# HGRN2's normed output copied by DMA into a tile typed as rounded fp32, transposed there, and the first heads' transposes placed behind the second heads' products

## The chip, the cores and the metric

The kernel runs on one core of a Trainium2 chip. The metric is the device time of one execution in microseconds (us); of several runs the median is given. The engines are named as the profile names them: PE (TensorE) multiplies, PEld is its load of the stationary operand, DVE (VectorE), ACT (ScalarE) and POOL (GpSimd) work on elements, and SP (SyncE) issues most of the DMAs. ACT and POOL issue DMAs too, and in such a case the profile writes ACTq or POOLq.

## The reference, cut to what matters

One decoder layer on 256 tokens of width 1024: two token mixers read one input projection, their outputs are projected, gated, added, projected again and normalised, and a feed-forward block follows. The change is in the first mixer, at the place where its output `o_a` is normed and gated and handed to `w_branch_a`:

```python
o_a = hgrn2_mixer(hq, hf, hi, lb)                     # B, S, 8 heads, 128
y_a = rms_norm(o_a, hgrn_norm_w) * silu(hg)           # per head
z_a = einsum('bsc,cd->bsd', y_a, w_branch_a)
z_b = einsum('bsc,cd->bsd', moba(...), w_branch_b)
mixed = einsum('bsc,cd->bsd', g_a * z_a + g_b * z_b, w_out)
```

## The kernel before

Large products are made of three: both operands are split into a high part, which is the value in the type of rounded fp32 (`F32R`, in the rows fp32r), and a low part, the rest. Weights arrive from HBM as tiles of 1024 KB (`raw`, issued by SP, L230), ACT casts the high part (`wh`, L236), DVE subtracts the low part (`wl`, L238), and PE uses both. Up to three tiles are staged ahead of their use. Beside them SP and POOL build sums of weights in HBM (`sums`, L246, L247, L252) for later products.

The tokens lie in two tiles of 128 (index `u`). The first mixer is a generator, `hgrn_steps`, and the second, attention, is one too (`moba_heads`); the big projections call `side.step()` at fixed places, and each call runs a generator up to its next `yield`. In this stretch the projections are `mk` and `mq` (keys and queries of the attention, `wide_pair`, L363 and L366: per step one product of 512 columns and one of 256), then `mv` (values, L423 to L425, 512 columns) and again `mk`. Which instruction of an engine comes first is decided at build time by a scheduler that estimates when operands are ready; on the chip every engine then works through its own list in order.

The end of `hgrn_steps` works on two groups `g` of four heads. For each group and token tile, plain fp32 products `o` (L661, L662; each shows as two records of PE) give the output, ACT squares it (`sq`, L664), DVE sums the squares and POOL takes the power -0.5 (L668), and DVE writes the normed and gated output `on` (L671). Then PE transposes `on`, 128 by 128, against the identity matrix `ident`, which lies in the tile of constants `cst` (`ot`, L680: 16 in all, eight for each group), and ACT and DVE make the high and low parts `yah` and `yal` with the norm's weights (L683, L684). Their only reader is `za`, the product with `w_branch_a`.

PSUM tiles come from two pools of four banks, `mm` for projections and `aux` for the rest. SBUF tiles of 1024 KB (`slot`) come from one pool of 12.

Of the kernel before, what the change touches and what calls it, by code (L numbers as in the profile page):

```python
# [10 lines left out]
F32 = mybir.dt.float32  # L11
F32R = mybir.dt.float32r
# [5 lines left out]
P = 128  # L18
T = 256
NT = T // P  # L20
# [115 lines left out]
def hybrid_layer_kernel(ctx: ExitStack, tc, x, xw, vecs, bias, wts, ln1_w, ln1_b, ln2_w, ln2_b, consts, out):  # L136
    nc = tc.nc
    pool = lambda name, bufs, **kw: ctx.enter_context(tc.tile_pool(name=name, bufs=bufs, **kw))
    cp = pool("cp", 1)
# [7 lines left out]
    aux = pool("aux", 4, space=PSUM)  # L147

    def slot(name, dt=F32):
        return big.tile([P, 2048], dt, tag="s8", name=name)  # L150

    def r32(ap):
        return ap.bitcast(F32)
# [166 lines left out]
    ident = cst[:, C_ID:C_ID + P]  # L320
# [2 lines left out]
    sin = cst[:, C_SIN:C_SIN + T]  # L323
    masks = msk.bitcast(U32).rearrange("p (l t) -> p l t", l=LEVELS)
    ones = cp.tile([P, P], F32R, tag="ones", name="ones")
    half = cp.tile([P, 4], F32, tag="half", name="half")

    nw = vec[:, 16:24]
# [204 lines left out]
    def hgrn_steps():  # L533
# [113 lines left out]
        for g in range(2):  # L647
# [2 lines left out]
                nc.tensor.matmul(ps[:, a, :], Kt[:, 0, 4 * g + a, :], Qt[:, 1, 4 * g + a, :], start=True, stop=True)  # L650
            nc.scalar.copy(SL[:, 4 * g:4 * g + 4, :], ps)
        yield
        on = slot("on").rearrange("p (t d) -> p t d", t=NT)
        for g in range(2):
            for u in range(NT):
                ps = aux.tile([P, 4, P], F32, tag="aux", name=f"o{g}{u}")
                for a in range(4):
                    h = 4 * g + a
                    hd = slice(h * P, (h + 1) * P)
                    if u == 1:  # L660
                        nc.tensor.matmul(ps[:, a, :], SL[:, h, :], hv[:, 0, hd], start=True, stop=False)  # L661
                    nc.tensor.matmul(ps[:, a, :], SD[:, u, h, :], hv[:, u, hd], start=(u == 0), stop=True)  # L662
                sq = sm.tile([P, 4, P], F32, tag="sg", name=f"sq{g}{u}")
                nc.scalar.activation(sq, ps, AF.Square)  # L664
                st = sm.tile([P, 12], F32, tag="ost", name=f"ost{g}{u}")
                nc.vector.reduce_sum(st[:, 0:4], sq, axis=mybir.AxisListType.X)
                nc.vector.tensor_scalar(st[:, 4:8], st[:, 0:4], 1.0 / P, RMS_EPS, op0=ALU.mult, op1=ALU.add)
                nc.gpsimd.tensor_tensor(st[:, 8:12], st[:, 4:8], half, op=ALU.pow)  # L668
                for a in range(4):
                    hd = slice((4 * g + a) * P, (4 * g + a + 1) * P)  # L670
                    nc.vector.scalar_tensor_tensor(on[:, u, hd], ps[:, a, :], st[:, 8 + a:9 + a], hgs[:, u, hd],  # L671
                                                   op0=ALU.mult, op1=ALU.mult)
            yield
            for j in range(2):
                h0 = 4 * g + 2 * j
                pt = aux.tile([P, 2, T], F32, tag="aux", name=f"ot{g}{j}")
                for a in range(2):
                    for u in range(NT):
                        hd = slice((h0 + a) * P, (h0 + a + 1) * P)
                        nc.tensor.transpose(pt[:, a, u * P:(u + 1) * P], on[:, u, hd], ident)  # L680
                for a in range(2):
                    h = h0 + a
                    nc.scalar.activation(yah[:, h, :], pt[:, a, :], AF.Copy, scale=nw[:, h:h + 1])  # L683
                    nc.vector.scalar_tensor_tensor(yal[:, h, :], pt[:, a, :], nw[:, h:h + 1], r32(yah[:, h, :]),  # L684
                                                   op0=ALU.mult, op1=ALU.subtract)
        yield

    class Steps:
# [15 lines left out]

    side = Steps()
    side.gens.append(hgrn_steps())
    side.step()

# [355 lines left out]
    def new_room():  # L1064
        return slot("room").rearrange("p (n b t) -> p n b t", n=2, b=8)
# [82 lines left out]
    with tc.manual_schedule(engines={ET.PE, ET.DVE, ET.Activation}):  # L1148
        a = new_room()
# [22 lines left out]
        d = new_room()  # L1172
# [70 lines left out]
        for i, q in enumerate(SEQUENCE):  # L1243
            if q in FAST:
                fast(q)
                if q == FAST[-1]:
                    with tc.issue_after(state["load"].ins):
                        wb2 = bcast("wb2", ln2_w, ln2_b, nc.sync)
                        unit = slot("unit")[:, 0:P]
# [131 lines left out]
```

## Time and profile before

| | |
|---|---|
| median of 3 runs | 484.13 us (484.08 to 484.2) |
| the profiled execution | 484.45 us, its span 482.6 us |
| PE busy | 476.5 us, 99% |
| DVE, ACT, POOL busy | 394.4, 302.9, 83.2 us |
| DMA moved | 131.31 MB, 272 GB/s |

The profiled execution's own time is 1.85 us longer than its span (what lies around the span) and 0.3 us above the median. A row of the timeline or of the chain begins with the start and the length in us from the start of the span.

### The profile page before, as it was taken

What the parts mean: (1) busy time and instruction counts of PE and PEld (TensorE: products, weight loads), DVE (VectorE), ACT (ScalarE), POOL (GpSimd) and SP (SyncE); (2) the same over time, 40 slices, a digit from 0 to 9 for tenths busy, and PEclk for the clock granted to TensorE, in tenths of its full rate; (3) what the DMA queues carried; (4) which work ended last, traced back from release to release, by engine and by line L of the source; (5) the groups of instructions that cost most, each with busy time, mean ns of one, the idle gap of its engine ahead of it and who ended that gap; (6) DMA issues with size and microseconds to landing.
All of it is one profiled execution on the core that took longest, in us unless ns stands there. A gap on an engine that the chain in (4) does not pass through costs nothing.

```text
span 482.6 us, 7450 instructions
## 1 busy us (share of the span) xinstructions
PE 476.5 (99%) x2915; PEld 406.7 (84%) x2915; DVE 394.4 (82%) x488; ACT 302.9 (63%) x408; POOL 83.2 (17%) x93
## 2 busy tenths in 40 slices
PE   9999999999999999999999999999999999999995
PEld 8888888788899888888888888888888888888884
DVE  4889895599977898999576678857797999889995
ACT  6699564454776677764934453643864876578744
POOL 0001111111008653440120210020010110000021
PEclk9999999999999999999999999999999999999999
DMA  8989989989699997959999986399499989789932
GB/s 301 414 304 324 292 241 270 321 249 246 208 368 238 271 239 230 235 132 338 317 267 313 289 237 244 125 316 356 173 313 320 263 294 308 242 305 379 411 99 88
DMA packets 29619, 131.31 MB, mean 272 GB/s; under 512 B 3344, under 2 KB 4752, under 8 KB 20112
## 3 DMA queue, kind: packets, MB, share of 16 engines
q1 hardware_dynamic: 20160, 113.66, 64.5%
q0 software_dynamic: 9136, 16.78, 21.6%
q8 instruction: 23, 0.38, 0.3%
q10 hardware_dynamic: 288, 0.39, 0.2%
q14 instruction: 12, 0.10, 0.0%
HBM read 128.72 MB, written 28.31 MB: 325 GB/s over the span
## 4 chain that ended last, share of the span: by engine, by line
PE 97%; DMA 1%; ACT 0%; DVE 0%; issue 0%; DVEq 0%; POOL 0%; POOLq 0%; SPq 0%; ACTq 0%
PE fu L363 5%; PE fg L363 5%; PE hq L363 3%; PE wp L1214 3%; PE wp L1215 3%; PE wp L1213 3%; PE fg L366 3%; PE fu L366 3%; PE mq L363 2%; PE mk L363 2%; PE gb L423 2%; PE mv L423 2%; PE hg L423 2%; PE hq L366 2%; PE hf L397 2%; PE ga L423 2%
## 5 line engine op out<-in xcount | busy, mean ns | idle before, releaser
L238 DVE TENSOR_TENSOR wl<-raw,wh 128x2048 fp32r<-128x2048 f32 (+1 forms) x65 | 149.0, 2297 | 42.3 <-ACT wh L236 42.0
L236 ACT CAST wh<-raw 128x2048 fp32r<-128x2048 f32 (+1 forms) x65 | 122.2, 1886 | 43.2 <-DMA raw<-in_wts_dram 18.5
L252 POOL DMA_DIRECT2D sums<-sums x26 | 21.4, 834 | 157.8 <-DMA sums<-in_wts_dram 80.2
L363 PE MATMUL fg<-x1p,wh 128*128 128x512 f32 x112 | 39.3, 395 | 0.0
L252 POOL DMA_DIRECT2D sums<-in_wts_dram x26 | 23.5, 1101 | 91.6 <-DMA sums<-in_wts_dram 91.5
L363 PE MATMUL fu<-x1p,wh 128*128 128x512 f32 x112 | 39.3, 395 | 0.0
L366 PE MATMUL fu<-x1p,wl 128*128 128x256 f32 x112 | 30.9, 278 | 0.0
L366 PE MATMUL fg<-x1p,wl 128*128 128x256 f32 x112 | 30.8, 278 | 0.0
L295 DVE TENSOR_TENSOR wlsums<-rawsums,whsums 128x2048 fp32r<-128x2048 f32 x11 | 25.2, 2289 | 6.3 <-ACT whsums L292 6.3
L292 ACT CAST whsums<-rawsums 128x2048 fp32r<-128x2048 f32 x11 | 21.1, 1917 | 8.2 <-PE wp L1215 4.9
L363 PEld LDWEIGHTS fu<-x1p,wh 128*128 128x128 f32 x112 | 20.9, 188 | 4.8
L363 PEld LDWEIGHTS fg<-x1p,wh 128*128 128x128 f32 x112 | 20.9, 188 | 4.6
L281 DVE TENSOR_TENSOR wlcorners<-rawcorners,whcorners 128x1536 fp32r<-128x1536 f32 x13 | 22.8, 1753 | 0.9 <-ACT whcorners L278 0.9
L363 PE MATMUL hq<-xp,wh 128*128 128x512 f32 x64 | 22.2, 394 | 0.0
L366 PEld LDWEIGHTS fg<-x1p,wl 128*128 128x128 f32 x112 | 21.1, 188 | 0.2
L366 PEld LDWEIGHTS fu<-x1p,wl 128*128 128x128 f32 x112 | 21.0, 188 | 0.1
L278 ACT CAST whcorners<-rawcorners 128x1536 fp32r<-128x1536 f32 x13 | 19.3, 1487 | 0.7
L366 PE MATMUL hq<-xp,wl 128*128 128x256 f32 x64 | 17.7, 277 | 0.0
L363 PE MATMUL mq<-xp,wh 128*128 128x512 f32 x48 | 17.0, 398 | 0.0
L363 PE MATMUL mk<-xp,wh 128*128 128x512 f32 x48 | 16.7, 395 | 0.0
L363 PEld LDWEIGHTS hq<-xp,wh 128*128 128x128 f32 x64 | 12.0, 188 | 2.8
L366 PE MATMUL mq<-xp,wl 128*128 128x256 f32 x48 | 13.2, 281 | 0.0
(413 smaller groups left out, 1381.2 us busy)
## 6 DMA issues: line engine op xcount, KB each, us to landing
raw<-in_wts_dram SPq DMA_DIRECT2D x63, 1024.0 KB, 7.8
sums<-in_wts_dram SPq DMA_DIRECT2D x26, 512.0 KB, 9.6
rawsums<-sums SPq DMA_DIRECT2D x11, 1024.0 KB, 6.7
rawcorners<-in_wts_dram SPq DMA_DIRECT2D x13, 768.0 KB, 7.3
sums<-in_wts_dram POOLq DMA_DIRECT2D x26, 256.0 KB, 9.9
sums<-sums POOLq DMA_DIRECT2D x26, 256.0 KB, 8.0
xw<-in_xw_dram SPq DMA_DIRECT2D x6, 640.0 KB, 9.0
raw<-sums SPq DMA_DIRECT2D x4, 512.0 KB, 7.3
```

The costliest lines, as they stand in the source:

```text
L236: nc.scalar.copy(h[:, ks, :], raw[:, ks, :])
L238: eng.tensor_sub(l[:, ks, :], raw[:, ks, :], r32(h[:, ks, :]))
L252: nc.gpsimd.dma_start(s[:, n, :], src, accum_op=ALU.add)
L278: nc.scalar.copy(h, b[:, 1:4, :])
L281: nc.vector.tensor_sub(l, b[:, 1:4, :], r32(h))
L292: nc.scalar.copy(h[:, bs, :], z)
L295: nc.vector.tensor_sub(l[:, bs, :], z, r32(h[:, bs, :]))
L363: nc.tensor.matmul(ps, wh[:, k, wcol], a.both(k), start=(k == 0), stop=False)
L366: nc.tensor.matmul(ps[:, 0, :], wl[:, k, wcol], a[0, k, slice(0, T)], start=False, stop=(k == KC - 1))
L423: nc.tensor.matmul(pss[t], ah[:, kk, ts], wh[:, k, :], start=(kk == 0), stop=False)
L1213: nc.tensor.matmul(ps, ah[:, a, :], wh[:, b, :], start=(q == begins[id(ps)]), stop=False)
L1214: nc.tensor.matmul(ps, ah[:, a, :], wl[:, b, :], start=False, stop=False)
```

## The change

The identity is copied once into a tile `unit_r` typed as rounded fp32. `on` is no longer the operand of the transposes: for each group and token tile a DMA issued by ACT copies its 128 by 512 elements word for word into a second tile `onr`, whose type is rounded fp32, and the transposes read `onr` and `unit_r` and write a PSUM tile of that type. The rows of the generator are cut in two functions. `outputs(0)` comes first, then a `yield`, then `outputs(1)` and `transposed(0)`, a `yield`, and `transposed(1)`.

```diff
+    unit_r = cp.tile([P, P], F32R, tag="unit", name="unitr")
...
+        nc.scalar.copy(unit_r, ident)
         on = slot("on").rearrange("p (t d) -> p t d", t=NT)
-        for g in range(2):
+        onr = slot("onr", F32R).rearrange("p (t d) -> p t d", t=NT)
+        def outputs(g):
             for u in range(NT):
                 ps = aux.tile([P, 4, P], F32, tag="aux", name=f"o{g}{u}")
...
-            yield
+                own = slice(4 * g * P, 4 * (g + 1) * P)
+                nc.scalar.dma_start(r32(onr[:, u, own]), on[:, u, own])
+
+        def transposed(g):
             for j in range(2):
                 h0 = 4 * g + 2 * j
-                pt = aux.tile([P, 2, T], F32, tag="aux", name=f"ot{g}{j}")
+                pt = aux.tile([P, 2, T], F32R, tag="aux", name=f"ot{g}{j}")
                 for a in range(2):
                     for u in range(NT):
                         hd = slice((h0 + a) * P, (h0 + a + 1) * P)
-                        nc.tensor.transpose(pt[:, a, u * P:(u + 1) * P], on[:, u, hd], ident)
+                        nc.tensor.transpose(pt[:, a, u * P:(u + 1) * P], onr[:, u, hd], unit_r)
+                pt = r32(pt)
...
+        outputs(0)
+        yield
+        outputs(1)
+        transposed(0)
+        yield
+        transposed(1)
         yield
```

The change moves instructions on PE, ACT and DVE; the lists of SP and POOL stay as they were. These are PE's instructions at the first group's transposes before (`mq` is the projection around them, `o` the second group's products):

```order
L680 MATMUL ot_1619<-cst,on 128x128 [waits DMAHW7_49,DVE_49]
L363 MATMUL mq_1695<-xp_97,wh_1390 128x512
L366 MATMUL mq_1695<-xp_97,wl_1391 128x256
L680 MATMUL ot_1628<-cst,on 128x128 [waits DVE_49]
L363 MATMUL mq_1695<-xp_97,wh_1390 128x512
L662 MATMUL o_1637<-hv,SD 128x128 [waits DVE_49,Activation_49]
L680 MATMUL ot_1619<-cst,on 128x128 [waits DVE_49]
L680 MATMUL ot_1619<-cst,on 128x128
```

And this is the same place of the change:

```order
L686 MATMUL ot_1660<-unitr,onr 128x128 [waits DMAHW1_49,DVE_49,Activation_49]
L686 MATMUL ot_1669<-unitr,onr 128x128 [waits DVE_49,Activation_49]
L364 MATMUL mq_1702<-xp_98,wh_1391 128x512
L367 MATMUL mq_1702<-xp_98,wl_1392 128x256
L364 MATMUL mq_1702<-xp_98,wh_1391 128x512
L686 MATMUL ot_1660<-unitr,onr 128x128 [waits DMAHW2_49]
L686 MATMUL ot_1660<-unitr,onr 128x128 x2
L686 MATMUL ot_1669<-unitr,onr 128x128 x3
L367 MATMUL mq_1702<-xp_98,wl_1392 128x256
L424 MATMUL mv_0_1749<-wh_1469,xp_97 128x512 [waits Activation_49]
```

The second group's products now stand as one block between `mk` and `mq`, ahead of this place, and the first transposes come after 14 of the 16 steps of `mq`, where it was ten. The first two wait for a DMA (the copy of token tile 0), the next six for another (token tile 1). The second group's eight stand in the next `mk` (behind all of `mv`), in the same form.

On ACT, at the same time in the program, the change has this, where before the two copies `rtk` followed `zk` directly:

```order
L781 COPY zk_1568<-mk_1594 128x256 [waits PE_49]
L677 DMA onr<-on 128x512 [waits DVE_49]
L677 DMA onr<-on 128x512 [waits DMAHW2_49,DVE_49]
L203 CAST keys<-kT 128x256 [waits PE_49]
L203 CAST keys<-kT 128x256
L786 COPY rtk_1615<-zk_1568 64x512 [waits DVE_49]
L787 COPY rtk_1615<-zk_1568 64x512
```

The two copies of the first group are issued one behind the other, and wait there for DVE's `on`. Those of the second group stand further on, one ahead of and one behind the cast of `mv`:

```order
L787 COPY rtq_1723<-zq_1678 64x512
L677 DMA onr<-on 128x512 [waits DVE_49]
L203 CAST mv<-mv_0_1749 128x512 [waits PE_49]
L677 DMA onr<-on 128x512 [waits DVE_49]
L236 CAST wh_1847<-raw_1846 128x2048 [waits DMAHW3_49,PE_49]
```

So the second of them is issued only when PE has finished the first half of `mv`. At the start of the program ACT also gets the copy of the identity, and it stands ahead of the copies that empty the first PSUM banks:

```order
L236 CAST wh_352<-raw_351 128x1024 [waits DMAHW5_49]
L654 CAST unitr<-cst 128x128 [waits DMAHW7_49]
L438 COPY Fg<-hf_145 128x2x128 [waits PE_49]
L438 COPY Fg<-hf_146 128x2x128 [waits PE_49]
L236 CAST wh_365<-raw_364 128x2048 [waits DMAHW6_49,Activation_49]
```

It waits for the DMA that brings the constants, which no instruction of ACT waited for at this place before.

## Rows read from the trace of the kernel before

**Rows 1.** The page: busy time of each engine, and the chain's shares.

```profile
PE 476.5 (99%) x2915; PEld 406.7 (84%) x2915; DVE 394.4 (82%) x488; ACT 302.9 (63%) x408; POOL 83.2 (17%) x93
PE 97%; DMA 1%; ACT 0%; DVE 0%; issue 0%; DVEq 0%; POOL 0%; POOLq 0%; SPq 0%; ACTq 0%
```

**Rows 2.** PE's waits, 5 to 470 us: total, times, longest.

```profile
PE hf L394 <- ACT fh L203: 0.2, 1, 0.2
```

**Rows 3.** Chain of work in order of time: start, us, what.

```profile
10.54 0.96 PE hf L400 x8
11.50 1.84 PE hf L397 x8
...
154.46 0.23 PE mq L363
...
158.97 0.66 PE ot L680 x6
159.62 0.67 PE o L662 x6
...
163.82 0.24 PE mv L424
...
228.84 0.23 PE za L424
```

**Rows 4.** The tile `ot`: duration min/median/max in ns, first and last start.

```profile
L680 PE MATMUL ot<-cst,on x16: 270/272/273, 157.8 to 174.7; 128*128 128x128 f32 x16
L684 DVE SCALAR_TENSOR_TENSOR yal<-ot,vec,yah x8: 473/476/483, 160.8 to 180.5; 128x256 fp32r<-128x256 f32 x8
```

**Rows 5.** Timeline of ACT, 140 to 186 us.

```profile
154.39 1.91 ACT L236 CAST wh<-raw 128x2048 fp32r<-128x2048 f32 x1 [0.62 <-PE mk L363]
156.19 0.37 ACT L767 COPY zk<-mk 128x256 f32<-128x256 f32 x1
...
171.83 0.59 ACT L203 CAST mv<-mv 128x512 fp32r<-128x512 f32 x1 [0.40 <-PE mv L425]
```

**Rows 6.** Timeline of DVE, 140 to 186 us.

```profile
154.22 2.16 DVE L671 SCALAR_TENSOR_TENSOR on<-o,ost,hgs 128x128 f32<-128x128 f32 x8
156.33 2.29 DVE L238 TENSOR_TENSOR wl<-raw,wh 128x2048 fp32r<-128x2048 f32 x1
...
168.12 2.15 DVE L671 SCALAR_TENSOR_TENSOR on<-o,ost,hgs 128x128 f32<-128x128 f32 x8
```

**Rows 7.** DMA issues, all and by stretch: KB each, us to landing.

```profile
out_dram<-z ACTq DMA_DIRECT2D x1, 256.0 KB, 2.3
...
sums<-in_wts_dram POOLq DMA_DIRECT2D x1, 256.0 KB, 6.1
...
sums<-in_wts_dram POOLq DMA_DIRECT2D x2, 256.0 KB, 9.6
```

**Rows 8.** Tile `z`: the one DMA that ACT issues at the end.

```profile
L1338 ACTq DMA_DIRECT2D out_dram<-z x1: 354/354/354, 478.5 to 478.5; - x1
```

**Rows 9.** Stretches: engines' busy us, granted clock, DMA share, GB/s.

```profile
core 0: us, PE busy (x) PEld busy (x) DVE busy (x) ACT busy (x) POOL busy (x), PEclk, DMA share, GB/s
155.00:160.00 5.00, 5.00 (x36) 4.57 (x35) 4.65 (x9) 2.56 (x4) 0.20 (x1) 1.00 0.96 317
...
170.00:175.00 5.00, 5.00 (x27) 4.14 (x27) 4.30 (x5) 2.35 (x3) 4.31 (x3) 1.00 1.01 276
175.00:180.00 5.00, 5.00 (x31) 4.40 (x30) 4.76 (x9) 4.98 (x9) 1.57 (x2) 1.00 0.92 264
```

**Rows 10.** The start: timelines of SP, ACT and DVE, and a landing.

```profile
12.04 0.33 SPq L492 DMA_DIRECT2D cst<-in_consts_dram  x1
...
cst<-in_consts_dram SPq DMA_DIRECT2D x1, 512.0 KB, 12.4
...
23.41 0.37 ACT L437 COPY Fg<-hf 128x256 f32<-128x256 f32 x1
...
24.71 0.75 DVE L438 TENSOR_TENSOR Fg<-hf,Fg 128x256 f32<-128x256 f32 x2
...
28.06 0.40 PE L363 MATMUL hq<-xp,wh 128*128 128x512 f32 x1
```

## The prediction

> **What bounds the kernel.** I read the page first: PE is busy 476.5 of 482.6 us, and the chain that ended last runs over PE for 97% [rows 1]. The list of waits then says that between 5 and 470 us PE stands still once, for 0.2 us [rows 2]. Throughout the stretch of the change its granted clock is 1.00, the level of 2.4 GHz [rows 9]. So the time moves by what PE's own instructions get shorter or longer, and by any wait that PE newly has. All other work counts only if it makes PE wait. DMA is the resource with the least room here: its engines are taken to 0.92 to 1.01 [rows 9].
>
> **What is removed: the price of 16 transposes.** Six in a row take 0.66 us of the chain, 0.110 us each; six records of the fp32 products `o`, also of 128 columns, take 0.67 us, the same [rows 3]. The new ones have both operands in rounded fp32. The trace has no product in that type as narrow as 128 columns. The nearest rows: eight of 512 columns take 1.84 us, eight of 256 columns 0.96 us, so 0.230 and 0.120 us each, near enough in proportion to the columns [rows 3]. By proportion 128 columns take 0.058 to 0.060 us. From above, a whole fp32 product of this size is two records, 0.22 us. Three cases then: 0.059 us (gain 16 x 0.051 = 0.82 us), no change (0), and 0.22 us (loss 1.8 us). I take 0.059, since a product in this type has shown its price by columns at both widths; the other two stay in the range.
>
> The load of the stationary operand is the doubt. Every one of the 256-column products above has its own load and they follow at 0.120 us, so the load takes no longer than that; whether it could follow at 0.06 no row shows. The Trainium skill (TensorE: Matmul & The Clock Gate, LDWEIGHTS) has a load of 128 columns take 128/1.2 = 107 ns; by it the transposes would stay near 0.11 us and the gain be 0.05 us. No run here shows a pair faster or slower than that at 128 columns.
>
> **What is added on the way to PE: four copies.** Before, a transpose needed DVE's `on`; now it needs a DMA that ACT issues behind it. I set up the clock of the first group. DVE writes its `on` in eight pieces from 154.22 to 156.38 [rows 6]. ACT comes to the first issue behind the cast at 154.39 and the copy at 156.19, so at about 156.5 [rows 5]; an issue from ACT takes it 0.354 us [rows 8], so the second copy is issued at about 156.9. PE ends `mk` and starts the next block at 154.46 [rows 3]. In the change that is the 24 records of `o`, 24 x 0.111 = 2.67 us, and then 14 steps of `mq` at 0.230 + 0.118 = 0.348 us, 4.87 us: the first two transposes come up at 162.0, and after two of them, two products of 512 and one of 256 columns, the next six at 162.75. So the first copy has 5.5 us to land and the second 5.9 us.
>
> The second group: in the old order the first product of `mv` stands one step of 0.23 ahead of the row at 163.82, so `mv` begins at 163.6 [rows 3]. I keep that, since the same work lies ahead of it but for half the gain, a shift that moves issue and need together. The copy of token tile 1 stands behind the cast of `mv`, which follows PE's first half of `mv`: it began at 171.83 and took 0.59 us [rows 5]. Issue at about 172.4. PE needs it after all 48 products of `mv` (48 x 0.230 = 11.0), 11 products of the next `mk` (2.0), two transposes and one attention score (0.7): 163.6 + 13.7 = 177.3. So it has 4.9 us. The copy of token tile 0 is issued when DVE's second `on`, at 168.12 [rows 6], is half done, and has some 7 us.
>
> How long does such a copy of 256 KB take? The one DMA of this size that ACT issues lands in 2.3 us, with nothing beside it [rows 7]. On a queue beside a loaded SP queue the nearest are POOL's of 256 KB around this stretch, 6.1 and 9.6 us [rows 7]; they add in HBM, which a plain copy doesn't. Worked out from the rate of the stretch, 317 GB/s with the engines at 0.96 [rows 9]: 262 kB alone is 0.8 us, which leaves 1.5 us of the 2.3 fixed. If ACT's and SP's queues share equally, a copy moves in 1.65 us and lands after 3.2 us, and the second, issued 0.35 us later and queued behind it, after 4.5 us: no wait. If SP's rows of 8 KB (1024 KB over 128 partitions) alternate with the copy's rows of 2 KB, it gets a fifth, 63 GB/s, 4.1 us for each: landings after 5.6 us and 9.4 us, and PE waits 0.1 us and then 3.5 us. Between these I take 4.5 and 6.7 us: a wait of **0.8 us** at the first group. At the second only one copy is under way at a time; equal shares give 1.5 + 1.9 = 3.4 us, a fifth gives 1.5 + 4.8 = 6.3 us at 276 GB/s, against 4.9 us of room. The value between is 4.85 us, just at the edge; as only lateness costs, I put down **0.2 us**. The wait is the same if it falls on the two transposes or the six, since PE works in order.
>
> **What is moved and costs nothing, with its cover.** ACT issues four DMAs, 4 x 0.354 = 1.4 us, and stands waiting for `on` at none of them long: it is free 2.4 of 5 us in the first stretch [rows 9]. Behind them are queued casts of keys, rope copies and the cast of a weight tile; the weight tile staged next to them was ready at 156.33 + 2.29 = 158.6 [rows 6] and is used after `mv`, 16 us later, so weights have that much room before PE sees it. `yah` and `yal` are done by 181 [rows 4] and first read at 228.84 [rows 3]: 48 us of cover for any lateness behind the transposes. The four copies add 1.05 MB of traffic, 3.3 us at 317 GB/s, to loads with that room of 16 us.
>
> The copy of the identity makes ACT wait for the constants. They were issued at 12.04 and land 12.4 us later, at 24.4; ACT came to the copies out of PSUM at 23.41 [rows 10]. So ACT stands 1.0 us and copies for 0.3 us, and all behind it is 1.3 us late. The first bank that PE needs again is freed by DVE at 24.71 + 0.75 = 25.5, then 26.8, and PE asks for it at 28.06 [rows 10]: 1.2 us are left. Without them it would cost what exceeds 28.06.
>
> **The sum.** -0.8 (transposes) + 0.8 + 0.2 (waits) = +0.2 us, on the profiled execution's 484.45 (span 482.6 and 1.85 around it), which stands 0.3 above the median; against the median of 484.13 that gives **484.3 us**. Less than 0.2%, 0.97 us, is about what a measurement here can't tell from no change.
>
> **The rivals.** *The copies land late, and the kernel is slower.* For it speaks how full DMA is [rows 9] and POOL's 6.1 and 9.6 us [rows 7]; against it, that the copies add nothing up and stay on the chip. With one landing time L for both copies that PE runs into, PE waits (L - 5.5) + (L - 4.9) us, and the loss outweighs the gain by over 0.97 us from L = 6.1 us on. At the fifth's share the waits are 3.6 + 1.4 = 5.0 us, less 0.8: 488.3. Middle of the case: 486.5 us.
>
> *The load sets the pace of a transpose.* The gain is then nothing, and the waits stay: 484.13 + 1.0 = 485.1 us, right at the edge of what can be told apart. For it speaks that fp32 records of 128 columns, each with a load, never come closer than 0.110 us [rows 3]; against it, that in fp32 the columns alone may explain this.
>
> *Rounded fp32 at 128 columns is as dear as the plain product*, 0.22 us: +1.8 + 1.0 = 486.9 us. Nothing in the trace speaks for it but that no such product is this narrow.
>
> *All goes well*: no wait and the whole gain, 483.3 us, which is still within 0.2%. To be faster by more, something besides must shrink on PE, and nothing else on PE is touched.
>
> **Chances.** The forecast (waits of up to 1.5 us, gain 0.8, so 483.3 to 484.8) 0.50; copies late 0.22; load sets the pace 0.15, half of it beyond the bound; the dear product 0.08; faster by over 0.2% 0.05. So faster 0.05, same 0.50 + 0.07 = 0.57, slower 0.38. The likeliest case alone spans 483.3 to 484.8; the range goes on through the load's and the dear product's times into the late copies, and is cut at 3.7 us of wait, with some 0.1 left out above and 0.05 below: 483.3 to 487.0 us.
>
> **What would show it.** In the profile after: the rows of `ot` at 0.06 us each in the chain (0.11: the load; 0.22: the product); a wait of PE on the DMA that writes `onr`, at about 162.75 and 177.3 us, in total 1 us; the landing times of four DMAs from ACTq, 4.5 to 6.7 us; ACT idle 1 us before the copy of the identity, and no wait of PE behind it. I am wrong if PE waits for `onr` over 2 us, if it waits at 28 us, or if another wait of PE appears where the attention's steps have been reordered behind this place.

## The result, and the profile after

The changed kernel takes 487.67 us, the median of twelve runs between 485.29 and 490.14; the kernel before took 484.10 in the same comparison (483.53 to 484.48). The ratio is 1.0072, with a 95% interval of 1.0053 to 1.0090: 3.5 us slower. As striking as the median is the spread, 4.9 us where it was 1.0 (the kernel before ranged over 3.8 us in the 100 later executions timed beside the experiments). The profiled execution happens to be the shortest of the twelve (485.29 us, span 483.5), so its trace shows the change at its mildest. I read it first, and then three more executions of the same kernel.

The page, PE's waits, and the chain of work in order of time (start, us, what) of that execution; they answer to [rows 1 to 3]:

```profile
PE 476.5 (99%) x2915; PEld 406.4 (84%) x2915; DVE 392.7 (81%) x488; ACT 304.1 (63%) x409; POOL 85.0 (18%) x93
PE 92%; DVE 3%; DMA 1%; ACT 1%; issue 0%; DVEq 0%; POOL 0%; POOLq 0%; ACTq 0%
```

```profile
PE ot L686 <- DMA onr<-on: 0.5, 1, 0.5
PE ga L424 <- DVE zk L782: 0.4, 1, 0.4
```

```profile
162.29 0.47 PE ot L686 x6
...
169.08 7.16 DMA onr<-on
...
176.37 0.38 PE ot L686 x2
...
201.32 0.35 DVE zk L782
201.71 0.50 PE ga L424
```

Six transposes take 0.47 us, 0.078 each, where they took 0.110 [rows 3]. But the product behind such a row starts late, as PE's timeline shows (start and length of the records, us):

```profile
161.36 0.28 PE L686 MATMUL ot<-unitr,onr 128*128 128x128 f32 x2
161.48 0.46 PE L364 MATMUL mq<-xp,wh 128*128 128x512 f32 x1
161.78 0.28 PE L367 MATMUL mq<-xp,wl 128*128 128x256 f32 x1
...
162.13 0.63 PE L686 MATMUL ot<-unitr,onr 128*128 128x128 f32 x6
162.60 0.35 PE L367 MATMUL mq<-xp,wl 128*128 128x256 f32 x1
162.79 0.40 PE L424 MATMUL mv<-wh,xp 128*128 128x512 f32 x1
```

From 161.36 to 161.78 two transposes and a product of 512 columns take 0.42 us; the product alone takes 0.23, so the two cost 0.19. By the same account the six cost 0.66 less 0.12. That is 0.73 us for eight, 0.091 each, and the gain of all 16 is 0.3 us, not the 0.5 that 0.078 gives.

PE waits for the second heads' rows once, at 176.37, for 0.5 us. The chain, which ran over PE alone, now passes through one copy of 7.16 us and, up to 201.7 us, through DVE and ACT: the attention steps have been reordered, and PE waits 0.4 us for `zk`. The first heads' copies land in this execution just in time, at 161.08 and 161.89 us for transposes that start at 161.36 and 162.13. The four copies, by the tile `onr` (issue in ns, then us to landing), against the guesses made from [rows 7, 8]:

```profile
L677 ACTq DMA_DIRECT2D onr<-on x4: 472/472/523, 154.9 to 171.2; - x4
DMA to landing us min/median/max: 5.7/6.1/7.2
```

### The profile page after: what moved, and what is told of

It reads as the page before. It is cut to its first block, busy times and chain, and to the rows that moved or that the text cites. A ratio compares the mean times of both kernels' runs of the same rounds, so it can differ in the third digit from the quotient of the medians.

```text
span 483.5 us, 7464 instructions
## 1 busy us (share of the span) xinstructions
PE 476.5 (99%) x2915; PEld 406.4 (84%) x2915; DVE 392.7 (81%) x488; ACT 304.1 (63%) x409; POOL 85.0 (18%) x93
## 4 chain that ended last, share of the span: by engine, by line
PE 92%; DVE 3%; DMA 1%; ACT 1%; issue 0%; DVEq 0%; POOL 0%; POOLq 0%; ACTq 0%
PE fu L364 5%; PE fg L364 5%; PE hq L364 3%; PE wp L1228 3%; PE wp L1227 3%; PE wp L1229 3%; PE fg L367 3%; PE fu L367 3%; PE hg L424 2%; PE ga L424 2%; PE gb L424 2%; PE hf L398 2%; PE hq L367 2%; PE ga L426 2%; PE za L425 2%; PE za L426 2%
## 5 line engine op out<-in xcount | busy, mean ns | idle before, releaser
L238 DVE TENSOR_TENSOR wl<-raw,wh 128x2048 fp32r<-128x2048 f32 (+1 forms) x65 | 146.9, 2265 | 47.2 <-ACT wh L236 46.9
L252 POOL DMA_DIRECT2D sums<-sums x26 | 21.4, 834 | 149.0 <-DMA sums<-in_wts_dram 75.4
L789 POOL TENSOR_TENSOR rtk<-rtk,cst 128x512 f32<-128x512 f32 x4 | 6.6, 1653 | 39.9 <-ACT rtk L787 29.8
```

The lines of the kernel that those rows point to most:

```text
L238: eng.tensor_sub(l[:, ks, :], raw[:, ks, :], r32(h[:, ks, :]))
L252: nc.gpsimd.dma_start(s[:, n, :], src, accum_op=ALU.add)
```

## The experiments

Times are medians; the kernel before was timed beside each group of runs. Before took 484.49 us beside the change again, the order alone, the unread copies and the rounding by DVE; 484.58 beside the lines moved, the two runs in the old order and half the bytes; 484.28 beside the calls from the loop, their control and the single executions `again_b` and `again_c`; 484.47 beside the last three.

### The change again, three more executions

The kernel is unchanged; each of the three gives the trace of another execution.

> The changed kernel once more, for another execution's trace. Its executions lie between 485.3 and 490.1 us, and the one profiled was the shortest. Late copies: a longer execution shows PE waiting for the moved rows (onr) by about as much as it is longer than 485.3 us, with landings over the 5.7 to 7.2 us of the first trace. Backlog of the new order: the extra time stands instead in PE's waits for DVE in the attention steps around 200 us (0.4 us in the first trace). Traffic: PE waits for weights or for projections' inputs somewhere behind 170 us. If the mean clock falls without a longer wait, none of the three.

> The changed kernel, one more execution and trace. Late copies: span less 482.9 us (no wait, transposes cheaper, 0.45 for the order) equals PE's waits on the moved rows plus half of the time at half clock, to within 1 us; and the longer waits go with the later landings (6 us: 0.5 us of wait, 9 to 10 us: 3.9 us).

> As the run before it, for a fourth execution: the same sum within 1 us.

Six executions, the first of the three among them, have a median of 489.04 us (486.57 to 492.42), ratio 1.0095 (1.0065 to 1.0125). The profiled executions took 492.42, 491.02 and 486.73 us. PE's waits in the first, the second and the third:

```profile
PE ot L686 <- DMA onr<-on: 3.9, 2, 2.5
```

```profile
PE ot L686 <- DMA onr<-on: 3.3, 2, 1.7
```

```profile
PE ot L686 <- DMA onr<-on: 1.2, 1, 1.2
```

The chain of the first of them shows what follows such a wait:

```profile
157.24 9.90 DMA onr<-on
167.18 1.00 PE ot L686 x6
...
168.52 0.43 PE mv L424
...
172.36 0.43 PE mv L424
173.58 0.23 PE mv L424
```

and its stretches (the columns of [rows 9]) show the clock:

```profile
160.00:165.00 5.00, 2.46 (x16) 1.95 (x15) 2.72 (x7) 2.21 (x4) 3.82 (x5) 1.00 1.03 408
165.00:167.00 2.00, 0.84 (x5) 0.48 (x4) 0.00 (x0) 1.12 (x1) 2.00 (x4) 0.89 0.88 272
167.00:169.00 2.00, 1.82 (x9) 1.72 (x10) 0.01 (x1) 1.94 (x5) 1.31 (x2) 0.50 0.84 141
169.00:171.00 2.00, 2.00 (x6) 1.52 (x6) 2.00 (x1) 0.23 (x1) 0.00 (x0) 0.50 1.04 129
171.00:173.00 2.00, 2.00 (x6) 1.53 (x5) 2.00 (x7) 0.87 (x2) 0.00 (x0) 0.50 0.64 123
173.00:175.00 2.00, 2.00 (x9) 1.64 (x8) 2.00 (x8) 0.00 (x0) 0.00 (x0) 0.91 0.99 340
```

PE was busy 3.3 of the 7 us from 160 to 167. Then the granted clock is 0.50, the level of 1.2 GHz, until about 173, and a product of 512 columns takes 0.43 us in place of 0.23. Busy time multiplied by the share of the clock that is missing gives 0.84 x 0.11 + 1.82 x 0.50 + 4.00 x 0.50 + 2.00 x 0.09 = 3.2 us lost. The second execution waits 3.3 us and loses 3.0 in the same way. The third waits 1.2 us and its clock stays at 1.00. The sum: the first trace without its wait has a span of 483.0; 483.0 + 3.9 + 3.2 = 490.1 (measured 490.5), 483.0 + 3.3 + 3.0 = 489.3 (489.1), 483.0 + 1.2 = 484.2 (484.8). Late copies account for the four executions to within 0.6 us. The base of 483.0 already holds the 0.4 us for `zk`, which all four have. I had expected the first repeat's excess over the shortest execution, 7.1 us, to be all wait; 3.4 us of it are, and 3.2 are the clock.

The clock is not what makes the middle executions slow. Those of 490.14, 490.09 and 489.03 us in the first comparison have a mean granted clock of 0.990 to 0.993, and the two traced ones with the half clock have 0.990. The other nine, up to 489.37 us, have 0.995 to 0.999, as the two traced ones without it (0.996). By the sum an execution at the median of 487.67 us, at full clock, would have waited some 2.8 us. That is an estimate: no execution between 486.73 and 491.02 us was traced.

### Order alone, copies that nobody reads, rounding without copies

The new order alone has no `onr`, no copies and no second identity:

```diff
-                nc.scalar.dma_start(r32(onr[:, u, own]), on[:, u, own])
...
-                        nc.tensor.transpose(pt[:, a, u * P:(u + 1) * P], onr[:, u, hd], unit_r)
+                        nc.tensor.transpose(pt[:, a, u * P:(u + 1) * P], on[:, u, hd], ident)
```

The copies that nobody reads have the second of these edits alone. For the rounding by DVE, the copies go and DVE's instruction writes `onr`:

```diff
-                    nc.vector.scalar_tensor_tensor(on[:, u, hd], ps[:, a, :], st[:, 8 + a:9 + a], hgs[:, u, hd],
+                    nc.vector.scalar_tensor_tensor(onr[:, u, hd], ps[:, a, :], st[:, 8 + a:9 + a], hgs[:, u, hd],
```

> Keeps the new order (second heads' products ahead of the first heads' transposes) and leaves out the copies, the second identity and the rounded type: the transposes read the normed output in fp32 as before. Late copies: no copy, so 484.0 to 484.6 us with a spread under 1 us. Backlog of the new order: as slow as the change, 486 to 488 us. Traffic: 484.0 to 484.6 us.

> New order and the four copies and the identity's copy are issued, but the transposes read the normed output itself in fp32, so nothing waits for a copy to land. Late copies: 484.0 to 484.8 us with a spread near 1 us. Traffic or the ACT queue's time for the issues: as slow as the change, 486 to 488 us. Backlog of the new order: 486 to 488 us too.

> Leaves out the copies: DVE writes the normed output into the place typed as rounded fp32 itself (so the normed output is rounded, which changes the computation), and the transposes are the rounded ones. Late copies: what the transposes gain without a wait, 16 x (0.110 - 0.078) = 0.5 us, so 483.3 to 484.0 us, with a spread under 1 us. Backlog of the new order, or rounded transposes that cost elsewhere: 486 to 488 us.

| | us | range | ratio (95%) | PE's waits behind 100 us |
| --- | --- | --- | --- | --- |
| order alone | 484.96 | 484.35 to 485.24 | 1.0008 (1.0000 to 1.0017) | `ga` 0.5 |
| copies unread | 485.61 | 484.83 to 487.07 | 1.0027 (1.0017 to 1.0038) | `ga` 0.5 |
| rounded by DVE | 484.26 | 484.07 to 485.30 | 1.0002 (0.9993 to 1.0011) | none but the last one, as before |
| the change | 489.04 | 486.57 to 492.42 | 1.0095 (1.0065 to 1.0125) | `ot` 3.9, `ga` 0.4 |

(Each list also has the 0.3 us of `wp` at the end of the program, which before has too.) With the copies issued but not read the time is 485.61; reading them adds 3.4 us (2.1 by the 487.67 of the first comparison), although the transposes get 0.3 us cheaper. So the wait with its aftermath costs some 2.4 to 3.7 us, and the order and the mere presence of the copies about 0.5 and 0.6. The runs differ from the change in the place too: the scheduler lets the first transposes start at 157.5 to 157.8 us in these three, and at 161.4 in the change.

The new order's 0.5 us fits the wait for `zk`. The 0.6 of the copies has no wait in the trace; that execution loses its time far behind the copies, where PE takes 93.3 us from the first `fu` to the first `wp` and 92.3 under the order alone. So its cause isn't shown. The third run does not isolate the transposes: its 0.70 us under the order alone is partly the wait for `zk`, which its trace doesn't have. A rounded transpose that stands there alone between wider products, as the one at 157.50 us, gains nothing: with the product of 512 columns behind it it takes 0.34 us, 0.11 more than that product alone.

### Moved later: once in vain, once really

Two edits put the transposes later. In the first, the lines change place but the scheduler decides: in PE's list the first transposes stand four instructions behind where the change has them, and the chip shows them at 162.9 us with two waits, 1.0 us in all. The second calls them from the attention heads' loop. A control has those late places without copies.

The lines moved:

```diff
         outputs(1)
+        yield
         transposed(0)
-        yield
         transposed(1)
```

Called from the loop of `moba_heads`, ahead of its steps 0 and 3:

```diff
         outputs(1)
-        transposed(0)
         yield
-        transposed(1)
+        put_off.extend([lambda: transposed(1), lambda: transposed(0)])
...
         for i in range(n + lags[-1]):
+            if i in (0, 3):
+                put_off.pop()()
```

> Copies and rounded transposes stay; the first heads' transposes are moved behind the values' products to where the second heads' stand, so their copies have some 16 us of PE work to land in instead of about 6. Late copies: the wait on the first heads' rows goes, the half clock behind it too; what is left is the order's 0.5 us, the traffic's 0.6 and at most the second heads' wait of some 0.5, less 0.5 from the transposes: 484.5 to 486 us, spread under 2 us. Traffic or the ACT queue as the main cause: as slow as the change, 487 to 489 us.

> The move behind the values' products that left the first transposes where they were, forced: both groups' transposes are called from the attention heads' loop, so that PE's list has 24 of the values' products (some 5.5 us) more ahead of the first group and 50 more instructions ahead of the second than in the changed kernel. Copies and rounded transposes stay. Late copies: no wait on the moved rows is left and no half clock, so the order's and the unread copies' cost less the transposes' gain, 484.5 to 485.6 us, spread under 2 us. If the copies cost by their traffic or by the ACT queue, or the wait only shows a stall that would stand anyway: 487 to 489 us as before.

> The same late places for both groups' transposes, in fp32 from the normed output itself, without copies and second identity: what this place costs by itself. Under late copies it stands 0 to 0.7 us above or below the run with the copies: 484.5 to 485.3 us. If it is 486 us or more, the late place has a cost of its own (DVE and ACT work pushed into the attention steps), and the run with the copies must be read against it.

Lines moved: 488.43 us (486.59 to 491.02), ratio 1.0082 (1.0054 to 1.0110), no better than the change, because almost nothing was moved. Called from the loop: **484.92 us**, ratio 1.0020 (1.0003 to 1.0036), eleven of twelve runs from 484.55 to 485.65 and one at 488.80, which stays unexplained. Its control: 484.28, ratio 1.0000 (0.9985 to 1.0014). In the trace of the run with copies, PE waits for nothing between 150 and 200 us and the clock stays at 1.00, though the copies land no earlier than in the change (7.0 and 7.6 us for the first heads, 8.9 and 9.5 for the second). Its copies, traffic and rounded transposes are those of the change; the room is larger, and the wait of 0.4 us for `zk` is gone as well. So each is compared with its own control: the copies cost 0.6 us here (484.92 less 484.28) and 2.7 to 4.1 us in the change (487.67 and 489.04 less the 484.96 of the order alone). Copies that land too late for PE are thus the cause of some 2.1 to 3.4 us, and traffic is not the main one.

### The old order with the copies, and with rounding by DVE

```diff
+        for g in range(2):
+            outputs(g)
+            yield
+            transposed(g)
+        yield
```

> Copies and rounded transposes, but the order of before (each group's transposes behind its own step). PE has about 2 us less to do ahead of each group's transposes than in the changed kernel. Late copies: longer waits on the moved rows, 2 to 6 us in all, with the half clock behind at least one: 488 to 494 us. Backlog of the new order as the main cause: faster than the change, 484 to 486 us.

> The order of before, no copies, DVE writes the normed output rounded (this changes the computation) and the transposes are the rounded ones: the gain of the transposes alone. 16 x (0.110 - 0.078) = 0.5 us if PE has them all on its path: 483.5 to 484.0 us. If the new order costs nothing and 484.3 us for the same with the new order is all there is: 484.1 to 484.5 us.

With the copies: 487.18 us (485.33 to 492.20), ratio 1.0067 (1.0036 to 1.0098). I expected longer waits than in the change; the trace of the profiled one (488.50) has 1.2 us for `onr` and 1.1 for `zk`, and the times overlap with the change's. But the run does not test less room, as the scheduler moved the transposes again:

```profile
162.84 0.40 PE L424 MATMUL mv<-wh,xp 128*128 128x512 f32 x1
163.07 0.29 PE L686 MATMUL ot<-unitr,onr 128*128 128x128 f32 x2
```

They stand behind all of `mq` and 13 products of `mv`, and start 7.5 us behind the first copy's issue at 155.62, where the change has 6.5. What the second heads' products bought by lying in between stays open. With rounding by DVE: 484.22 us, 0.9993 (0.9983 to 1.0004). The gain of the rounded transposes by themselves, some 0.1 to 0.3 us when the late products behind them are counted, is too small to be told from no change.

### Half the bytes in as many rows

```diff
-                own = slice(4 * g * P, 4 * (g + 1) * P)
+                own = slice(4 * g * P, (4 * g + 2) * P)
```

> As the run with copies that nobody reads, but each copy moves only two of its four heads: 128 KB in as many rows, each 1 KB instead of 2 KB (the transposes read the normed output in fp32). If a copy's landing goes by its bytes' share of the engines: from a median of 6.3 us to about 4. If its rows take turns with the weights' packets one by one: still about 6 us. For the time: 485.0 us if the bytes are the 0.6 us that the unread copies cost over the new order alone, 485.6 if it is the issues or the rows.

485.40 us (484.95 to 487.06), ratio 1.0020 (1.0007 to 1.0033). The landings of 128 KB were 5.2 to 10.7 us with a median of 8.5; whole copies unread had 4.9 to 7.2 and 6.3. Half the bytes landed no sooner. The other transfers of this stretch ran later here: POOL issued its loads at 148.4 us, against 146.0 in the run with whole copies. The fairer comparison is the repeat of 492.42 us, with POOL's loads at 149.0, whose first two whole copies took 8.5 and 9.9 us against 9.4 and 10.7 here. So the share of bytes, on which my estimate rested, does not set the landing; that the number of rows does isn't shown either. By time neither size of copy can be told from the other.

### What holds the copies back

Over the traces and with some scatter, the first heads' copies take the longer to land the later POOL had issued the two accumulating loads of `sums` that run ahead of them. The test takes those two loads out, with a control.

```diff
-BETWEEN = {"k0": ((21, 0),), "k1": ((21, 1), (23, 0)), "q1": ((21, 2), (23, 1)),
+BETWEEN = {"k1": ((21, 1), (23, 0)), "q1": ((21, 2), (23, 1)),
```

> The changed kernel without the two accumulating loads that POOL issues some 8 us ahead of the first copies (one block of weights is then missing in a sum, which changes the computation). If these loads hold back SP's 2 MB, behind which the copies land: the first copies land within 6 us in every execution seen, PE waits for them less than 0.5 us, no half clock, and the time is that of the unread copies less the transposes' gain, 484.3 to 485.6 us, spread under 2 us. If the copies' landing has nothing to do with them: 487 to 489 us and landings of 6 to 10 us as before.

> The control: the new order with fp32 transposes and no copies, also without the two accumulating loads (the same change of the computation). It gives what the loads' absence is worth by itself: 484.5 to 485.1 us, as with them, if nothing else on the path waits for those transfers; 483 us or so if their removal frees something.

The DMA issues of the stretch 154 to 158 us (KB each, median us to landing), of the first repeat and of the kernel without the two loads, where SP's 512 KB load had been issued at 151.96:

```profile
sums<-in_wts_dram SPq DMA_DIRECT2D x1, 512.0 KB, 13.0
onr<-on ACTq DMA_DIRECT2D x2, 256.0 KB, 9.2
```

```profile
onr<-on ACTq DMA_DIRECT2D x2, 256.0 KB, 2.9
```

From the issue times and landings of five traces, us (SP's last is the second 512 KB load of `sums`, issued 4.8 to 5.0 us ahead of the second copy):

| execution | POOL's loads issued | SP's last load lands | second copy issued | it lands | PE waits for the first heads |
| --- | --- | --- | --- | --- | --- |
| no early loads | none | 158.3 | 156.75 | 159.5 | 0 |
| the change, 485.29 | 145.3 | 161.3 | 155.92 | 161.9 | 0 |
| 486.73 | 146.3 | 163.2 | 156.65 | 164.2 | 1.2 |
| 491.02 | 147.1 | 164.4 | 155.86 | 165.8 | 3.3 |
| 492.42 | 149.0 | 165.2 | 157.24 | 167.1 | 3.9 |

The second copy lands 0.6 to 2.0 us behind SP's older load in all five, while that load itself took from 6.3 to 13.6 us. The first copy, issued 1.0 us ahead of the second and 4 us behind that load, lands 0.2 to 1.4 us before it in the four executions with POOL's loads, and 0.5 to 1.9 us behind the 512 KB load that SP issued just ahead of it. So a copy does not land behind all that was issued earlier. Without POOL's loads the second copy lands 2.7 us after its issue, and PE waits only for the second heads, 0.7 us. The excess over the control is 0.9 us (486.48, 485.95 to 488.63, ratio 1.0051, 1.0030 to 1.0071; control 485.60, 1.0019, 1.0003 to 1.0034), against 2.7 to 4.1 us with the loads (487.67 and 489.04 less 484.96). Both medians and the spread are above what was expected. The trace of the first has the waits of `onr` and `ga`, 1.1 us, which the removal doesn't touch, and a `hq` wait of 0.5 that the others don't have; the control's has 0.5 for `hf`. The executions above 487 us were not traced. Why POOL issues these loads at 145 us in one execution and at 149 in another was not followed.

On a DMA's end the Trainium skill (DMA: Bandwidth & Descriptors, Queues, rings and completion order) says that the write to the semaphore lands only behind the earlier writes of the same engine, across its queues. The second copies of the five rows agree with that order; the first copies show that the order of issue alone doesn't decide, and no run here separates the rule from a plain wait for a turn.

### A version from what was learnt

> The late places of both groups' transposes, no copies, DVE writes the normed output rounded (which changes the computation) and the transposes are the rounded ones. The late place cost nothing (484.3 us, as before) and the rounding by DVE gained 0.7 us over fp32 transposes in the new order: 483.5 to 484.0 us, if the two add. No measurable gain, 484.1 to 484.5 us, if PE's 0.5 us come back in another wait.

485.13 us (483.90 to 486.45), ratio 1.0011 (0.9997 to 1.0026). The two gains did not add, and nothing here beats the kernel before. The profiled execution has 0.8 us of an unexplained stop at `hg`, far ahead of the change; whether that is what lifts the median isn't shown.

## Why the prediction failed, point by point

**What bounds the kernel** held: PE is busy 476.5 us in the profiled execution before and after, and the losses that the traces explain are waits of PE or its clock.

**The price of a transpose** was mis-sized: 0.091 us for 0.059 with the late product behind each row counted, so 0.3 us of gain for 0.8. The rival in which a transpose stays at 0.11 us came true by half: it does so where it stands alone, and in rows of two and six, each with its own load of 128 columns, it costs 0.091. The Trainium skill (TensorE: Matmul & The Clock Gate, LDWEIGHTS) has such a load take 107 ns; the rows are below that, the single transpose is not.

**The landing of the copies is the step that failed.** The prediction set ACT's issues at 156.5 and 156.9; they came at 154.89 and 155.92, each right behind the half of DVE's `on` that it copies (`on` was written from 153.74 to 155.89). ACT's timeline shows the first issue while the cast still ran, and ahead of the `zk` copy that stands before it in ACT's list:

```profile
153.91 1.90 ACT L236 CAST wh<-raw 128x2048 fp32r<-128x2048 f32 x1 [0.62 <-PE mk L364]
154.89 0.52 ACTq L677 DMA_DIRECT2D onr<-on  x1
155.71 0.37 ACT L781 COPY zk<-mk 128x256 f32<-128x256 f32 x1
155.92 0.47 ACTq L677 DMA_DIRECT2D onr<-on  x1
```

Each issue took 0.47 to 0.53 us for the 0.354 assumed. The need at 162.0 and 162.75 was right within 0.7 us: 161.36, and 162.13 for the next six. So the room was larger than reckoned, 6.5 and 6.2 us, and the copies still came late in all but the mildest traced execution, because "between these I take 4.5 and 6.7" priced a landing by shares of bandwidth. The runs showed 6.0 to 9.9 us for the first heads' copies, set by loads that were under way when the copy was issued: 2.7 and 3.0 us without the two of POOL. The second copy's 9.4 us at a fifth's share was near the worst one, by another mechanism. The shares and the unloaded landing (2.6 to 3.1 us where the engines' share was 0.30 to 0.56 over the copy's own time, 2.3 taken) could not give it.

**One value for a wait that differs from run to run.** The trace of before is one execution; in it POOL's loads and SP's happened to cost nothing, since nobody waited for them. It did hold the sign: SP's second load of `sums`, issued at 151.38,

```profile
sums<-in_wts_dram SPq DMA_DIRECT2D x1, 512.0 KB, 12.6
```

landed at 164.0, behind the 162.75 at which PE was reckoned to need the second copy. With hindsight, 0.6 to 2.0 us behind that load makes a wait of 1.9 to 3.3 us, an estimate from this row and the five traces. With the copies PE inherits these loads' variation, and the spread of twelve executions goes from 1 us to 5.

**What a wait costs was left out.** The sum counted a microsecond of waiting as one. Behind the waits of 3.3 and 3.9 us PE's clock stood at half for some 7 us, which cost 3.0 and 3.2 us more; behind those of 0.5 and 1.2 us it stayed whole. This explains the longest executions, not the median, whose neighbours have the full clock.

**Work moved at no cost** was not free, but small: 0.5 us for the new order, by the wait for `zk` at 201.7 us, and about 0.6 that came with the copies, by a cause not shown. The identity's copy was free: ACT waited 1.7 us for the constants, until 23.99, and PE has no wait at 28 us.

**The rivals.** "The copies land late" is what happened, at 0.22 where it deserved the most. Its middle of 486.5 us lacked the order's 0.5 us and, for the longest executions, the clock. Its threshold was set at a landing of 6.1 us; the second copy of the mildest execution took 6.0 and had 6.2 us of room.

## What to carry to other kernels

A transfer that is put on PE's path can be held back by what is already under way, so look for the loads issued ahead of it and for when each of them lands, not for the engines' mean busy share or for a bare transfer of the same size. When such a wait is possible, price its worst execution, not its middle, and add the clock that PE loses behind it. A place in the code is not a place in the engine's list: check the list before a move is taken as an experiment, and in the controls too. Price a short product with the start of the one behind it, not by its own records.

## What the hardware showed unexpectedly

A copy of 256 KB took 2.6 to 9.9 us from issue to landing in one and the same program. Two accumulating loads of 256 KB each, issued by POOL 7 to 10 us earlier, made the difference for the first heads' copies: in the one trace without them it was 2.7 and 3.0 us beside the same loads of SP, at 409 GB/s in 156 to 158 us. While those loads ran, the engines counted as busy and moved little: in the change's profiled execution the stretch of 148 to 152 us has a DMA share of 1.01 at 88 GB/s:

```profile
148.00:152.00 4.00, 4.00 (x26) 3.52 (x26) 3.45 (x5) 2.00 (x4) 3.03 (x2) 1.00 1.01 88
156.00:160.00 4.00, 4.00 (x27) 3.57 (x27) 3.74 (x5) 2.20 (x6) 0.17 (x1) 1.00 1.03 391
```

A busy share of 1.0 thus stood for 88 and for 391 GB/s within 12 us. And a transpose in rounded fp32 with 128 columns costs 0.091 us in rows of two and six, half as much again as the proportion of the wider products in that type, [rows 3], gives, and 0.11 us alone; part of that price stands in the late start of the product behind it.
